# Stacks made by halves, gelus tied to a later split, and two slabs' low parts on VectorE in the differential-attention layer

## The chip, the cores and the metric

The kernel runs on one core of a Trainium2 chip. The metric is the device time of one execution in microseconds (us). PE is TensorE (matrix products), DVE is VectorE, ACT is ScalarE, POOL is GpSimd, and SP is SyncE, which issues the transfers.

## The reference

Two layers over 512 tokens and 256 context tokens, 768 in all, of width 1024. The change lies in the first ("even") layer. After an adaptive norm, `h` is projected into gate streams `u` and `v`, and into queries, keys and values of four heads. The heads are differential: two softmaxes of 64-wide queries and keys are subtracted, and each head's output is normed.

```python
u, v, q, k, vv = jnp.split(h @ w_in, [A_WIDTH, 2 * A_WIDTH, KV_START, KV_START + B_QK_WIDTH], axis=-1)

def diff_attn(q, k, v, lam):
    s = jnp.einsum('bqhd,bkhd->bhqk', q, k).astype(jnp.float32) * ATTN_SCALE
    p = jax.nn.softmax(s, axis=-1).reshape(b, B_HEADS, 2, tq, tk)
    a = p[:, :, 0] - lam * p[:, :, 1]
    return jnp.einsum('bhqk,bkhe->bqhe', a.astype(v.dtype), v)

def diff_out(o, g, lam_init):
    return (rmsnorm(o, g) * (1.0 - lam_init)).reshape(b, t, B_V_WIDTH)
```

The gate branch gives `gelu(u) * mixed(gelu(v))`. Both branches, side by side 1024 wide, go through the output projection `w_out`, and a gated MLP follows. The second ("odd") layer has windowed attention.

## The kernel before

All products are float32 to nearly full precision. Each operand is kept as a high part (a rounded copy, made by ScalarE) and a low part (what is left, a subtraction), and each product is three matmuls: high by high, high by low, low by high (`mm3`, lines 115 to 117). So every operand of PE needs a "split": `split` (L131 the copy on ScalarE, L132 the subtraction on VectorE or GpSimd) for activations, `unit` (L89 the copy, L92 the subtraction) for weights.

`even()` first makes queries, keys and values. Then come the four heads, t = 0 to 3. Each is made by `head(t)` in three passes, qp = 0, 1, 2, over 256 query rows each: `softmax_diff` computes the scores (L546, L547, into the two PSUM buffers of `wide`, called pw), takes the exponential on ScalarE (L550, with row sums) and subtracts the two maps on VectorE; `attend` transposes the map (L567), splits it (tiles ath, atl) and multiplies by the values; ScalarE copies the result into `o` (L579).

Queries and keys of a head are stacked: 64 rows of a high part over 64 of a low part, so that one matmul does the work of two. `stack(t)` made the query stacks (`stack_q`, L272 to L278, tiles qa and qb; the low parts of head 3 on GpSimd) and the key stacks (`stack_k`, L286 to L288, tiles kh and kl) in one go, called in the middle of the previous head, after its pass qp = 1.

While a head's softmax runs on the other engines, PE is filled with projections into a spare PSUM buffer (pf): `block` makes the queries and keys of the heads to come, `gated` the gate streams u, copied to SBUF by L588.

`norm(t, step)` is a head's RMS norm in three steps: squares (L640, tile sq), row sums by PE (L612) and a chain of small VectorE operations on six columns that ends in a diagonal matrix (`head_diag`, L615 to L627, tile q), and a spread of it over all rows (PE, L195) by which `o` is multiplied. For t < 3 the steps lie inside the next head; for head 3 they follow at once.

Behind the heads comes the output projection. `slab(n)` loads 128 rows of its weights (512 KB), in the order of `order = [4, 5, 6, 0, 1, 2, 3, 7]`: heads 0 to 2, the four gate streams, head 3. Slabs 0 and 1 are loaded ahead. The activations `cat[k]` are made by the gelu of a gate stream (k < 4, L671), the multiply by the mixed v, and the split. `project` runs eight slabs over eight 128-column blocks.

A list scheduler with a timeline of its own sets the order of each engine's instructions. `tc.issue_after(x)` makes an instruction stand behind x; `high_priority` puts the heads ahead of the fillers. Before the change `gelu(k)` for k < 4 was tied to the last exponential, `self.last_exp`.

Of the kernel before, what the change touches and what calls it, by code (L numbers as in the profile page):

```python
# [6 lines left out]
F32 = mybir.dt.float32  # L7
F32R = mybir.dt.float32r
# [3 lines left out]
ALU = mybir.AluOpType  # L12
AX = mybir.AxisListType.X

P = 128
# [4 lines left out]
TA = TX + TC  # L20
# [7 lines left out]
class Builder:  # L28
# [99 lines left out]

    def split(self, hi, lo, src, lo_eng=None):
        nc = self.nc  # L130
        nc.scalar.copy(hi, src)  # L131
        return (lo_eng or nc.vector).tensor_tensor(lo, src, hi.bitcast(F32), ALU.subtract)  # L132

    def rstd_small(self, ms, n, inv, tag):
# [133 lines left out]
    def stack_q(self, q, pool, T, tag, bufs, s=1.0, eng=None, out=None):  # L268
# [8 lines left out]
            else:  # L277
                nc.vector.scalar_tensor_tensor(lo[Y], q[X], s, hi[X].bitcast(F32), ALU.mult, ALU.subtract)  # L278
        return qa, qb

    def stack_k(self, k, pool, T, tag, bufs, lows):
        nc = self.nc
        out = []
        for X, Y, kl in zip((slice(0, 64), slice(64, 128)), (slice(64, 128), slice(0, 64)), lows):
            kh = pool.tile([P, T], F32R, name=self.uid("kh"), tag=tag, bufs=bufs)
            nc.scalar.copy(kh[X], k[X])  # L286
            nc.scalar.copy(kh[Y], k[X])
            nc.vector.tensor_tensor(kl[X], k[X], kh[X].bitcast(F32), ALU.subtract)  # L288
            out.append((kh, kl))
        return out  # L290


    def build(self):
# [37 lines left out]
    def even(self):  # L331
        tc, nc, a = self.tc, self.nc, self.a
# [9 lines left out]
        def f3(tag="f3", bufs=4):  # L342
            return R1.tile([P, TA], F32, name=self.uid(tag), tag=tag, bufs=bufs)
# [4 lines left out]
        for k in range(0, KT, 2):  # L348
            t = self.load(Rh, a["xT"][k * P:(k + 2) * P, :].rearrange("(k p) t -> p k t", p=P), [P, 2, TX], f"hx{k}")
# [47 lines left out]
        sq = self.squares(hx, TX)  # L397
# [24 lines left out]
        qk = {}  # L422
# [38 lines left out]
        for k in range(KT):  # L461
            t = self.adap.tile([P, 2, 512], F32R, name=self.uid("wq"), tag="wq", bufs=2) if k in (2, 5) else None
# [8 lines left out]
            t, sh = hx[k], self.modcol(0, 0, k, 0)  # L471
# [31 lines left out]
        for k in range(KT):  # L503
            W = self.unit(a["v0"][k * P:(k + 1) * P, :], 512)
            for tb in range(6):
                c = slice(tb * P, (tb + 1) * P)
# [25 lines left out]
        Ra = tc.alloc_tile_pool(name="att0", bufs=1, side="right", reuse_waits="tile")  # L532
        oraw, raw = [], {}

        def softmax_diff(Q, K, qb, sums):


            koff = 0 if qb < 4 else TX
            qs = slice(qb * P, (qb + 1) * P)
            nm, sums = self.small(2, "sa", 10), sums[:, 2 * qb:2 * qb + 2]  # L540
            es = []
            for c in range(2):
                ps = self.wide()
                for p in range(2):
                    if qb < 4:
                        nc.tensor.matmul(ps[:, :TX], Q[c][:, qs], K[c][p][:, :TX], start=p == 0, stop=p == 1)  # L546
                    nc.tensor.matmul(ps[:, TX:TA], Q[c][:, qs], K[c][p][:, TX:], start=p == 0, stop=p == 1)  # L547
                nc.vector.tensor_reduce(nm[:, c:c + 1], ps[:, koff:TA], axis=AX, op=ALU.max, negate=True)
                e = Ra.tile([P, TA], F32, name=self.uid("e"), tag="e", bufs=6)
                self.last_exp = nc.scalar.activation(e[:, koff:], ps[:, koff:TA], AF.Exp, bias=nm[:, c:c + 1],  # L550
                                                     accum_out=sums[:, c:c + 1])
                es.append(e[:, koff:])
            r = self.small(1, "sa", 10)
            nc.vector.reciprocal(r, sums[:, 1:2])
            nc.vector.scalar_tensor_tensor(r, r, self.nlam, sums[:, 0:1], ALU.mult, ALU.mult)
            nc.vector.scalar_tensor_tensor(es[0], es[1], r, es[0], ALU.mult, ALU.add)
            return es[0]

        def attend(t, Q, K, qp, o, eps):
            es = [softmax_diff(Q, K, 2 * qp + i, eps) for i in range(2)]  # L560
            kbs = list(range(6)) if qp < 2 else [4, 5]
            po = self.bank()[:, :TC]
            for i in range(0, len(kbs), 2):
                pt = self.bank()
                for j in range(2):
                    for b in range(2):
                        nc.tensor.transpose(pt[:, j * TC + b * P:j * TC + (b + 1) * P],  # L567
                                            es[b][:, (i + j) * P:(i + j + 1) * P], self.ident)
                th = Ra.tile([P, 512], F32R, name=self.uid("ath"), tag="at", bufs=6)
                tl = Ra.tile([P, 512], F32R, name=self.uid("atl"), tag="at", bufs=6)  # L570
                self.split(th, tl, pt)
                for j in range(2):
                    kb = kbs[i + j]
                    c = slice(t * P, (t + 1) * P)
                    m = slice(j * TC, (j + 1) * TC)
                    self.mm3(po, (vhi[kb][:, c], vlo[kb][:, c]), (th[:, m], tl[:, m]),
                             i + j == 0, i + j == len(kbs) - 1)
            s = slice(qp * TC, (qp + 1) * TC)
            nc.scalar.copy(o[:, s], po)  # L579

        def gated(i, after=None):

            W = self.blocks(a["uv"][i])
            u = f3() if i < 4 else f3("rv")
            for off, T, A in ((0, TX, axx), (TX, TC, axc)):
                ps = (self.fill if off or i < 4 else self.bank)()[:, :T]
                self.dense(ps, W, A, after, 0 if off else (2, 5)[i == 3])
                nc.scalar.copy(u[:, off:off + T], ps)  # L588
            raw[i] = u

        lows = [[Ra.tile([P, TA], F32R, name=f"kl{i}{c}") for c in range(2)] for i in range(2)]
# [1 line left out]
            nc.gpsimd.memset(lows[i][0][64:128].bitcast(F32), 0.0)  # L593
            nc.gpsimd.memset(lows[i][1][0:64].bitcast(F32), 0.0)

        def stack(t):
            return (self.stack_q(qk[t], Ra, TA, "sq", 3, eng=nc.gpsimd if t == 3 else nc.vector),
                    self.stack_k(qk[4 + t], Ra, TA, "kh", 3, lows[t % 2]))

        norms = {}  # L600

# [31 lines left out]
        def norm(t, step):  # L633

            if t not in norms:
                return
            o, eps = norms[t][:2]
            if step == 0:
                sq = self.sumsq()
                nc.scalar.activation(sq, o, AF.Square)  # L640
                norms[t] = o, eps, sq
            elif step == 1:
                sq = norms[t][2]
                norms[t] = o, eps, head_diag(sq, eps)
            else:
                for off, T, dg in ((0, TX, norms[t][2][0]), (TX, TC, norms[t][2][1])):
                    c = o[:, off:off + T]
                    nc.vector.scalar_tensor_tensor(c, c, self.subg, self.spread(dg), ALU.mult, ALU.mult)

        def head(t):  # L650
            Q, K = QK.pop(t)
            o = f3("o", 4)
            eps = self.small(12, "sx", 2)
            for qp in range(3):
                attend(t, Q, K, qp, o, eps)
                if qp == 0:
                    norm(t - 1, 1)
                elif qp == 1:
                    if t < 3:
                        QK[t + 1] = stack(t + 1)  # L660
                    norm(t - 1, 2)
            norms[t] = o, eps
            norm(t, 0)
            if t == 3:
                norm(t, 1)
                norm(t, 2)
            oraw.append(o)

        def gelu(i, after=None):
            with tc.issue_after(after.ins) if after else ExitStack():  # L670
                return nc.scalar.activation(raw[i], raw[i], AF.Gelu)  # L671
# [34 lines left out]
        def block(n):  # L706
# [7 lines left out]
                evacuate(ps, key, c)  # L714
            self.rope(qk[key][:, :TX], qk[key][:, :TX], tabs)

        QK = {0: stack(0)}
        for g in range(4):
            gated(4 + g)
            last = gelu(4 + g)  # L720
# [11 lines left out]
        for t, jobs in enumerate(((block, 0, 1), (block, 2, 3), (gated, 0, 1), (gated, 2))):  # L732
            for i in jobs[1:]:
                jobs[0](i, *([self.last_exp] if t == 3 else []))
            with tc.high_priority(offset=tc.cur_priority - here), tc.issue_after(last.ins):
                head(t)
        gated(3, self.last_sum)
        Ra.release()
        self.ropep.release()
        self.sh_bufs = 2  # L740
# [9 lines left out]
        def slab(n):  # L750
            k = order[n]
            Ws[k] = self.blocks(a["even_out"][k * P:(k + 1) * P, :], t=slots.pop())

        slab(0)
        slab(1)
        cat = {}
        for k in order:
            if k < 4:
                gelu(k, self.last_exp)
                nc.vector.tensor_tensor(raw[k], raw[k], raw[4 + k], ALU.mult)  # L760
            src = raw[k] if k < 4 else oraw[k - 4]
            cat[k] = self.ax()
            self.split(*cat[k], src, nc.gpsimd if k in (5, 6) else nc.vector)
        Rv.release()
        R1.release()

# [14 lines left out]
        sq, rest = self.sumsq(), []  # L781
# [1088 lines left out]
```

## Time and profile before

| | |
|---|---|
| Three runs | 1573.76, 1575.87 and 1576.09 us; median 1575.87 us |
| Profiled execution | 1582.97 us, of which its span is 1581.2 us |
| PE busy | 1516.2 us, 96% of the span, 9563 matmuls |
| DVE, ACT, POOL busy | 1072.9, 726.4, 828.9 us |
| Stretch of the heads and the first projection weights | about 120 to 360 us of the span |
| Granted clock of PE | 0.99 from 450 us on |

The span is the profiled core's program, and 1.8 us of the profiled time lie around it. A profiled run is one execution; here it lies 7.1 us above the median of the runs. "Granted clock" is the share of full speed that PE's clock had, and "busy" is time in which an instruction was executing.

### The profile page before, as it was taken

The numbers are of one execution on the slowest core, as the hardware profiler recorded it, in microseconds if no ns is written. First come the engines' busy times: TensorE is split into PE (matmuls) and PEld (weight loads), VectorE is DVE, ScalarE is ACT, GpSimd is POOL, SyncE is SP. The second block draws the span as 40 slices with busy tenths as digits, with TensorE's granted clock in tenths as the row PEclk, the third lists the DMA queues.
The fourth block names the chain that finished last, engine by engine and source line by source line (L and its number), as shares of the span: only waits on it lengthen the run. The fifth ranks groups of instructions, "written<-read, shape, count | busy, mean of one in ns | idle before, by whom it ended". The sixth has DMA issues, their size and how long they took to land.

```text
span 1581.2 us, 24961 instructions
## 1 busy us (share of the span) xinstructions
PE 1516.2 (96%) x9563; PEld 1357.0 (86%) x9563; DVE 1072.9 (68%) x1886; ACT 726.4 (46%) x1489; POOL 828.9 (52%) x562
## 2 busy tenths in 40 slices
PE   6999999889999999999999999899999999999998
PEld 4667888779999999999999988777869889999997
DVE  3612778773697787888886487665657976666665
ACT  2415565642562333333333354565655644444444
POOL 0453322051337767767776544531314299898982
PEclk9999999989999999999999999999999999999999
DMA  9762100042123333345442212210224133333301
GB/s 349 293 238 76 44 21 1 1 157 109 68 70 105 108 118 126 128 135 171 163 159 91 81 41 62 69 31 14 68 91 176 53 97 105 99 106 105 99 21 54
DMA packets 53415, 162.26 MB, mean 103 GB/s; under 512 B 6192, under 2 KB 8624, under 8 KB 45616
## 3 DMA queue, kind: packets, MB, share of 16 engines
q1 hardware_dynamic: 46240, 135.37, 25.5%
q10 hardware_dynamic: 7056, 25.30, 4.9%
q8 instruction: 75, 1.23, 0.3%
q14 instruction: 44, 0.36, 0.1%
HBM read 158.55 MB, written 2.10 MB: 102 GB/s over the span
## 4 chain that ended last, share of the span: by engine, by line
PE 84%; DVE 10%; ACT 3%; issue 2%; DMA 0%; POOL 0%; DVEq 0%; SPq 0%; ACTq 0%; POOLq 0%
PE pw L115 11%; PE pw L116 11%; PE pw L117 11%; PE pb L115 9%; PE pb L116 9%; PE pb L117 9%; PE pf L115 4%; PE pf L116 4%; PE pf L117 4%; PE pb L1680 2%; PE pb L1669 2%; PE pf L370 2%; PE pw L1631 1%; PE pw L1639 1%; DVE t L49 1%
## 5 line engine op out<-in xcount | busy, mean ns | idle before, releaser
L92 POOL TENSOR_TENSOR w<-raw,w 128x512 fp32r<-128x512 f32 (+1 forms) x78 | 115.4, 1484 | 239.5 <-ACT w L89 184.2
L116 PE MATMUL pw<-ax,w 128*128 128x384 f32 (+2 forms) x716 | 227.2, 318 | 4.7 <-DVE ax L473 2.5
L828 DVE SCALAR_TENSOR_TENSOR xT<-pb,mod,xT 128x512 f32<-128x512 f32 (+3 forms) x204 | 143.1, 708 | 129.2 <-PE pb L117 128.9
L115 PE MATMUL pw<-ax,w 128*128 128x384 f32 (+2 forms) x716 | 225.9, 318 | 3.6 <-DVE q L49 1.9
L117 PE MATMUL pw<-ax,w 128*128 128x384 f32 (+2 forms) x716 | 227.0, 317 | 0.1
L49 POOL TENSOR_TENSOR w<-raw,w 128x512 fp32r<-128x512 f32 x122 | 186.1, 1541 | 48.5 <-ACT w L49 48.4
L49 POOL TENSOR_TENSOR w<-t,w 128x512 fp32r<-128x512 f32 x99 | 148.1, 1499 | 56.2 <-ACT w L49 56.2
L115 PE MATMUL pb<-hh,w 128*128 128x512 f32 x480 | 171.2, 357 | 2.3 <-DVE xT L828 2.3
L117 PE MATMUL pb<-hh,w 128*128 128x512 f32 x480 | 171.7, 358 | 0.4 <-DVE w L49 0.4
L116 PE MATMUL pb<-hh,w 128*128 128x512 f32 x480 | 171.3, 357 | 0.0
L115 PE MATMUL pw<-T,w 128*128 128x384 f32 (+1 forms) x508 | 157.4, 311 | 2.5 <-DVE hs L1036 1.2
L116 PE MATMUL pw<-T,w 128*128 128x384 f32 (+1 forms) x508 | 157.7, 311 | 1.2 <-DVE T L132 1.2
L117 PE MATMUL pw<-T,w 128*128 128x384 f32 (+1 forms) x508 | 157.6, 311 | 0.0
L115 PE MATMUL pf<-ax,w 128*128 128x256 f32 (+2 forms) x460 | 150.6, 327 | 1.8 <-DVE qf L264 1.1
L116 PE MATMUL pf<-ax,w 128*128 128x256 f32 (+2 forms) x460 | 149.6, 325 | 0.0
L117 PE MATMUL pf<-ax,w 128*128 128x256 f32 (+2 forms) x460 | 149.3, 325 | 0.0
L116 PEld LDWEIGHTS pw<-ax,w 128*128 128x128 f32 x716 | 136.2, 190 | 9.6 <-DVE ax L473 3.4
L115 PEld LDWEIGHTS pw<-ax,w 128*128 128x128 f32 x716 | 135.5, 190 | 8.2 <-DVE q L49 2.6
L117 PEld LDWEIGHTS pw<-ax,w 128*128 128x128 f32 x716 | 136.1, 190 | 2.4 <-DVE w L999 0.4
L49 POOL TENSOR_TENSOR hh<-hs,hh 128x768 fp32r<-128x768 f32 (+1 forms) x42 | 78.1, 1860 | 94.8 <-ACT hh L49 69.1
L49 POOL TENSOR_TENSOR w<-rawo,w 128x512 fp32r<-128x512 f32 x59 | 104.0, 1762 | 29.5 <-ACT w L49 29.5
L240 DVE SCALAR_TENSOR_TENSOR junk<-ar,cb 128x1024 bf16<-128x1024 f32 x64 | 106.7, 1667 | 0.0
(429 smaller groups left out, 3924.9 us busy)
## 6 DMA issues: line engine op xcount, KB each, us to landing
raw<-ffn_in SPq DMA_DIRECT2D x44, 1024.0 KB, 5.1
ar<-ada SPq DMA_DIRECT2D x24, 1024.0 KB, 7.1
ar<-ada ACTq DMA_DIRECT2D x48, 512.0 KB, 3.6
rawo<-ffn_out SPq DMA_DIRECT2D x88, 256.0 KB, 3.0
raw<-odd_out SPq DMA_DIRECT2D x28, 256.0 KB, 2.6
raw<-qk SPq DMA_DIRECT2D x16, 256.0 KB, 4.6
raw<-uv SPq DMA_DIRECT2D x16, 256.0 KB, 3.4
raw<-even_out SPq DMA_DIRECT2D x8, 512.0 KB, 3.6
```

The source lines that it names most:

```text
L49: self.tail[key] = fn(*args, **kw)
L92: eng.tensor_tensor(lo, raw, hi.bitcast(F32), ALU.subtract)
L115: mm(out, s[0], m[0], start=start, stop=False, **kw)
L116: mm(out, s[0], m[1], start=False, stop=False, **kw)
L117: return mm(out, s[1], m[0], start=False, stop=stop, **kw)
L240: return self.nc.vector.scalar_tensor_tensor(junk, t, 1.0, self.cb[who], ALU.mult, ALU.mult, accum_out=self.acc[who][:, col:col + 1])
L370: nc.tensor.matmul(ps[32 * q:32 * q + 32, :w], cst[:, k, :], t[:, w * q:w * q + w], start=k == 0, stop=k == KT - 1, skip_group_check=True)
L828: ins = self.nc.vector.scalar_tensor_tensor(h, ps[:, r], self.modcol(l, j, m, who), h, ALU.mult, ALU.add)
L1631: nc.tensor.matmul(ps[:, st:en], Q, K[g][p][:, b0 * P:b1 * P], start=p == 0, stop=p == 1, skip_group_check=True)
L1639: last = nc.tensor.matmul(ps[:, en:en + TC], Q, K[g][p][:, TX:], start=p == 0 and not edge, stop=p == 1, skip_group_check=True)
L1669: last = nc.tensor.transpose(pt[:, x * P:(x + 1) * P], es[2 * (x % 2) + x // 2][:, kb * P:(kb + 1) * P], self.ident)
L1680: nc.tensor.matmul(po[64 * h:64 * h + 64, :], V[vb][:, 64 * g:64 * g + 64], t[:, h * TC:h * TC + TC], start=kb == 0, stop=kb == nb - 1, sk ...
```

## The change

Three things change in `even()`.

1. `stack_q` and `stack_k` are no longer used there. `stack(t, c)` makes one half, c = 0 or 1, of a head's query and key stacks: three copies on ScalarE (two of keys, one of queries) and two subtractions on VectorE. Half 0 is made in pass qp = 1 of the head before and half 1 in qp = 2, in `attend`, between the softmaxes and the products with the values. All low parts are VectorE's now, head 3's queries too.
2. The gelus for k < 4 are tied to the high part of the split for k = 6 (head 2's output), and the multiplies to the end of `head_diag` of head 3 and to the low part of the split for k = 4.
3. The weights' low parts of slabs 0 and 1 are made by VectorE instead of GpSimd (`self.dve_lo = 1`).

```diff
     def split(self, hi, lo, src, lo_eng=None):
         nc = self.nc
-        nc.scalar.copy(hi, src)
+        self.last_hi = nc.scalar.copy(hi, src)
...
             es = [softmax_diff(Q, K, 2 * qp + i, eps) for i in range(2)]
+            if qp and t < 3:
+                stack(t + 1, qp - 1)
             kbs = list(range(6)) if qp < 2 else [4, 5]
...
-        def stack(t):
-            return (self.stack_q(qk[t], Ra, TA, "sq", 3, eng=nc.gpsimd if t == 3 else nc.vector),
-                    self.stack_k(qk[4 + t], Ra, TA, "kh", 3, lows[t % 2]))
+        def stack(t, c):
+
+            q, k, low = qk[t], qk[4 + t], lows[t % 2][c]
+            X, Y = (slice(0, 64), slice(64, 128))[::1 - 2 * c]
+            qs = Ra.tile([P, TA], F32R, name=self.uid("qs"), tag="sq", bufs=3)
+            kh = Ra.tile([P, TA], F32R, name=self.uid("kh"), tag="kh", bufs=3)
+            nc.scalar.copy(kh[X], k[X])
+            nc.scalar.copy(qs[X], q[X])
+            nc.scalar.copy(kh[Y], k[X])
+            nc.vector.tensor_tensor(qs[Y], q[X], qs[X].bitcast(F32), ALU.subtract)
+            nc.vector.tensor_tensor(low[X], k[X], kh[X].bitcast(F32), ALU.subtract)
+            QK.setdefault(t, []).append((qs, (kh, low)))
...
-                    if t < 3:
-                        QK[t + 1] = stack(t + 1)
                     norm(t - 1, 2)
...
         gated(3, self.last_sum)
+        rooted = self.last_diag
...
+        self.dve_lo = 1
         slab(0)
         slab(1)
+        self.dve_lo = 0
         cat = {}
         for k in order:
             if k < 4:
-                gelu(k, self.last_exp)
-                nc.vector.tensor_tensor(raw[k], raw[k], raw[4 + k], ALU.mult)
+                gelu(k, after)
+                with tc.issue_after(rooted.ins), tc.issue_after(low.ins):
+                    nc.vector.tensor_tensor(raw[k], raw[k], raw[4 + k], ALU.mult)
             src = raw[k] if k < 4 else oraw[k - 4]
             cat[k] = self.ax()
-            self.split(*cat[k], src, nc.gpsimd if k in (5, 6) else nc.vector)
+            ins = self.split(*cat[k], src, nc.gpsimd if k in (5, 6) else nc.vector)
+            if k == 4:
+                low = ins
+            elif k == 6:
+                after = self.last_hi
```

The edit shortens the file ahead of `even()`, so lines behind it carry other numbers in the changed kernel (L550 becomes L539, L579 becomes L570, L671 becomes L669).

ScalarE, at the end of head 3's last pass (qp = 2): e is the exponential, f a gate stream, o the head's output, ath the high part of a transposed map, ax an activation of the projection. Before:

```order
L550 ACTIVATE e_3004,sx_2765<-pw_3000,sa_2993 128x256
L671 ACT_TABLE_LOAD
L671 ACTIVATE f_386_2306<-f_386_2306 128x768
L671 ACTIVATE f_393_2369<-f_393_2369 128x768
L671 ACTIVATE f_476_2711<-f_476_2711 128x768
L579 COPY o_2764<-pb_2808 128x256
L131 CAST ath_2929<-pb_2924 128x512
```

The same place after the change, and behind it the place where the gelus stand now:

```order
L539 ACTIVATE e_3004,sx_2765<-pw_3000,sa_2993 128x256
L570 COPY o_2764<-pb_2808 128x256
L131 CAST ath_2929<-pb_2924 128x512
```

```order
L131 CAST ax_3152<-o_1634 128x768
L131 CAST ax_3156<-o_2017 128x768
L131 CAST ax_3160<-o_2422 128x768
L669 ACT_TABLE_LOAD
L669 ACTIVATE f_386_2306<-f_386_2306 128x768
L669 ACTIVATE f_393_2369<-f_393_2369 128x768
L669 ACTIVATE f_476_2711<-f_476_2711 128x768
L579 COPY f_564_3071<-pf_3098 128x256
L89 CAST w_3138<-raw_3200 128x1024
```

The table load and three gelus have moved from ahead of the copy of `o` to behind the splits of heads 0 to 2, and ahead of the cast of slab 2.

VectorE, in head 3's norm (sm are its small columns, w the weights of a slab). Before:

```order
L615 SCALAR_TENSOR_TENSOR sm_3029<-pb_3033,sm_3031 128x4
L615 SCALAR_TENSOR_TENSOR sm_3029<-pb_3039,sm_3031 128x2
L616 TENSOR_SCALAR sm_3030<-sm_3029 128x6
L617 TENSOR_TENSOR sm_3031<-sm_3030 128x6
L618 SCALAR_TENSOR_TENSOR sm_3031<-sm_3031,sm_3029 128x6
```

After:

```order
L615 SCALAR_TENSOR_TENSOR sm_3029<-pb_3033,sm_3031 128x4
L92 TENSOR_TENSOR w_3143<-raw_3144,w_3143 128x1024
L615 SCALAR_TENSOR_TENSOR sm_3029<-pb_3039,sm_3031 128x2
L616 TENSOR_SCALAR sm_3030<-sm_3029 128x6
L92 TENSOR_TENSOR w_3142<-raw_3148,w_3142 128x1024
L617 TENSOR_TENSOR sm_3031<-sm_3030 128x6
L618 SCALAR_TENSOR_TENSOR sm_3031<-sm_3031,sm_3029 128x6
```

Two low parts of weights stand between the small operations; GpSimd's list no longer has them.

PE, behind the last filler matmuls (pf) that stand between heads 2 and 3; kh, kl, qb and qs are stacks, pb_2588 is head 2's product with the values, pb_2682 head 3's. Before:

```order
L115 MATMUL pf_3072<-ax_321,w_3068 128x512
L116 MATMUL pf_3072<-ax_322,w_3068 128x512
L117 MATMUL pf_3072<-ax_321,w_3068 128x512
L546 MATMUL pw_2890<-kh_2638,qb_2629 128x512
L547 MATMUL pw_2890<-kh_2638,qb_2629 128x256
L546 MATMUL pw_2890<-kl_1044,qb_2629 128x512
L547 MATMUL pw_2890<-kl_1044,qb_2629 128x256
L115 MATMUL pb_2682<-ath_2688,vhi_1022 128x256
```

After:

```order
L115 MATMUL pf_3072<-ax_321,w_3068 128x512
L116 MATMUL pf_3072<-ax_322,w_3068 128x512
L117 MATMUL pf_3072<-ax_321,w_3068 128x512
L116 MATMUL pb_2588<-atl_2610,vhi_1014 128x256
L117 MATMUL pb_2588<-ath_2609,vlo_1015 128x256
L115 MATMUL pb_2588<-ath_2609,vhi_1018 128x256
L116 MATMUL pb_2588<-atl_2610,vhi_1018 128x256
L117 MATMUL pb_2588<-ath_2609,vlo_1019 128x256
L535 MATMUL pw_2882<-kh_2582,qs_2581 128x512
L536 MATMUL pw_2882<-kh_2582,qs_2581 128x256
```

The fifteen filler matmuls stood behind head 3's first scores (pw_2882); they now stand ahead of them and of most of the rest of head 2. The order of `odd()` and of the two MLPs is the same in both kernels.

More of the change, by code (lines that the diff above doesn't have):

```diff
@@ L279, in stack_q @@
         return qa, qb
[L281 to L290, printed above, removed]
     def build(self):
@@ L650, in head @@
         def head(t):
-            Q, K = QK.pop(t)
+            Q, K = zip(*QK[t])
             o = f3("o", 4)
@@ L715, in block @@
             self.rope(qk[key][:, :TX], qk[key][:, :TX], tabs)
-        QK = {0: stack(0)}
+        QK = {}
+        for c in range(2):
+            stack(0, c)
         for g in range(4):
```

## The prediction

> **What bounds the kernel now.** The page comes first: it tells which engine ends last.
>
> ```profile
> span 1581.2 us, 24961 instructions
> PE 1516.2 (96%) x9563; PEld 1357.0 (86%) x9563; DVE 1072.9 (68%) x1886; ACT 726.4 (46%) x1489; POOL 828.9 (52%) x562
> PE 84%; DVE 10%; ACT 3%; issue 2%; DMA 0%; POOL 0%; DVEq 0%; SPq 0%; ACTq 0%; POOLq 0%
> ```
>
> TensorE is busy 96% of the span and makes 84% of the chain that ended last. The change adds and removes no matmul, so it can only act where TensorE waits, or runs at a lowered clock after a wait. The waits of PE in 120 to 450 us, which hold all that the change touches, come next (total, times, longest):
>
> ```profile
> PE pw L546 <- ACT e L550: 5.7, 4, 2.6
> PE pb L115 <- ACT ath L131: 4.7, 3, 3.8
> PE pb L195 <- DVE q L627: 4.2, 1, 4.2
> ```
>
> Then the busy times by stretch (length, then PE, PEld, DVE, ACT, POOL; granted clock; DMA share; GB/s):
>
> ```profile
> 245.00:255.00 10.00, 7.41 (x39) 6.42 (x38) 9.67 (x20) 7.05 (x14) 2.07 (x1) 0.83 0.00 0
> 255.00:300.00 45.00, 44.98 (x291) 40.14 (x290) 33.90 (x68) 26.43 (x57) 5.15 (x3) 1.00 0.00 1
> 300.00:312.00 12.00, 10.91 (x74) 9.06 (x72) 9.37 (x25) 8.07 (x20) 0.00 (x0) 1.00 0.01 1
> 312.00:315.90 3.90, 0.08 (x2) 0.01 (x1) 2.82 (x9) 3.83 (x6) 0.00 (x0) 0.86 0.01 2
> 315.90:323.10 7.20, 7.20 (x31) 6.11 (x32) 4.84 (x11) 1.41 (x3) 0.00 (x0) 0.60 0.00 0
> 334.20:338.45 4.25, 0.02 (x1) 0.00 (x0) 4.15 (x5) 1.80 (x3) 3.26 (x2) 1.00 0.76 271
> 338.45:342.04 3.59, 3.58 (x10) 2.38 (x10) 2.52 (x5) 0.00 (x0) 0.00 (x0) 0.54 0.31 122
> 342.04:360.00 17.96, 17.96 (x105) 17.96 (x105) 11.53 (x6) 10.88 (x13) 15.87 (x6) 1.00 0.66 223
> ```
>
> Two holes stand out, 312.0 to 315.9 and 334.2 to 338.45. Behind each the granted clock is low: 0.60 over 7.20 us and 0.54 over 3.59 us, which is 7.20 × 0.40 = 2.9 and 3.59 × 0.46 = 1.65 us of work lost. From 342.04 on PE is full.
>
> **Part A: the gelus leave the front of ScalarE.** The timeline of the first hole (start, duration):
>
> ```profile
> 311.28 0.19 ACT L550 ACTIVATION_READ_ACCUMULATOR e<-pw,sa 128x1 f32 x1
> 311.47 0.60 PE L567 MATMUL pb<-ident,e 128*128 128x128 f32 x4
> 311.49 1.28 ACT L671 ACT_TABLE_LOAD   x1
> 312.78 2.31 ACT L671 ACTIVATE f<-f 128x768 f32<-128x768 f32 x3
> 315.00 0.35 ACT L579 COPY o<-pb 128x256 f32<-128x256 f32 x1
> 315.25 0.59 ACT L131 CAST ath<-pb 128x512 fp32r<-128x512 f32 x1
> 315.89 0.58 PE L115 MATMUL pb<-ath,vhi 128*128 128x256 f32 x1 [3.82 <-ACT ath L131]
> 316.42 0.68 DVE L132 TENSOR_TENSOR atl<-pb,ath 128x512 fp32r<-128x512 f32 x1
> 323.10 0.60 PE L567 MATMUL pb<-ident,e 128*128 128x128 f32 x4
> ```
>
> The last exponential ends at 311.47; then ScalarE loads the gelu table and runs three gelus, and only afterwards casts the transposed weights for which PE stands. With the gelus tied behind the third split of the output projection, the transposes end at 312.07 and the cast (0.59) releases PE at about 312.75. The wait falls from 3.82 to 0.7 (−3.1). At full clock the 7.20 us shrink by up to 2.9 more, but VectorE is next late: three low parts at 0.68, four small operations and two of L627's before the transposes of 323.10 put these at about 318.0 instead of 317.1, so 0.9 to 1.0 is taken back. A = −3.1 − 2.9 + 0.9 = **−5.1**; bounds −3.1 (no clock comes back) and −6.0.
>
> Shorter waits stand at the starts of two earlier heads:
>
> ```profile
> 212.87 0.79 PE L546 MATMUL pw<-kh,qa 128*128 128x512 f32 x1 [1.94 <-ACT e L550]
> 249.83 0.70 PE L546 MATMUL pw<-kh,qa 128*128 128x512 f32 x1 [2.59 <-ACT e L550]
> ```
>
> The clock was 0.83 in 245 to 255, around the wait of 2.59, so a wait of that length costs clock too; the 0.7 that is left in A is far below it.
>
> [...]
>
> **Part B: VectorE makes the first slabs' low parts.** The second hole, head 3's norm:
>
> ```profile
> 328.49 0.16 DVE L615 SCALAR_TENSOR_TENSOR sm<-pb,sm 128x4 f32<-128x4 f32 x1 [3.44 <-PE pb L612]
> 328.54 4.74 POOL L92 TENSOR_TENSOR w<-raw,w 128x1024 fp32r<-128x1024 f32 x2 [42.92 <-PE pb L612]
> 329.13 1.84 DVE L616 TENSOR_SCALAR sm<-sm 128x6 int32<-128x6 int32 x1
> 331.00 2.29 DVE L617 TENSOR_TENSOR sm<-sm 128x6 f32<-128x6 f32 x1
> 333.33 0.17 DVE L618 SCALAR_TENSOR_TENSOR sm<-sm,sm 128x6 f32<-128x6 f32 x1
> 333.88 3.58 POOL L132 TENSOR_TENSOR ax<-o,ax 128x768 fp32r<-128x768 f32 x2 [0.61 <-ACT ax L131]
> 333.93 1.78 DVE L621 SCALAR_TENSOR_TENSOR sm<-sm,sm 128x6 f32<-128x6 f32 x1
> 335.75 1.73 DVE L622 SCALAR_TENSOR_TENSOR sm<-sm 128x6 f32<-128x6 f32 x1
> 337.71 1.03 DVE L627 SCALAR_TENSOR_TENSOR q<-sm,ident 128x512 f32<-128x512 f32 x2
> 338.45 1.86 PE L195 MATMUL pb<-q,ones 128*128 128x512 f32 x2 [4.23 <-DVE q L627]
> ```
>
> Operations on six columns that take 0.17 elsewhere take 1.84, 2.29, 1.78 and 1.73 while POOL makes a low part: 7.64 − 4 × 0.17 = 7.0 us of blocking on the chain for which PE waits 4.23. With the two slabs' lows on VectorE the first two of these blocks go, and the chain is done before POOL turns to the splits' lows at 333.88. What VectorE pays is bounded by
>
> ```profile
> L288 DVE TENSOR_TENSOR kl<-f,kh 64x768 fp32r<-64x768 f32 x8 | 7.6, 949 | 0.5 <-ACT kh L286 0.3
> L92 POOL TENSOR_TENSOR w<-raw,w 128x1024 fp32r<-128x1024 f32 x8 | 21.5, 2708 | 49.6 <-PE pb L612 42.9 <-ACT w L89 6.6
> ```
>
> VectorE's own subtraction scaled to 1024 columns gives 0.949 × 1024/768 = 1.27 each; POOL's price is 2.71. I take 1.27, the row of the engine that does it. From 328.49: ten small operations (2.0), two lows (2.5) and L627's first (0.7) end at 333.7. PE reaches the spreads at about 334.5, because the order puts them behind the last filler block (334.2) and two projection matmuls (17.96/105 = 0.17 each). So the wait of 4.23 goes, and the 1.65 of clock with it: B = **−5.9**. At POOL's price the chain ends at 333.7 + 2 × 1.44 = 336.6, 2.1 is waited, and B = −(4.23 − 2.1) − 1.65 = −3.8.
>
> [...]
>
> **Part C: the heads' order moves.** The stacks made in halves change PE's order: the last fifteen filler matmuls stand 21 attention matmuls earlier, so the stretch of attention alone is 21 × 44.98/291 = 3.2 us longer. In 300 to 312, with no filler, 12.00 − 10.91 = 1.09 was idle, which scales to 0.3; one whole wait like the 2.59 above is the other end. I take +1.0, between 0 (no gain, since 255 to 300 was full already) and 2.5. Head 3's two query lows go from POOL to VectorE, two at the 0.949 of the row above (the same shape). VectorE is busy 33.9 of 45 there and PE waits for none of it, so 0; if that cover were gone it would cost 1.9.
>
> **Part D: the halves themselves.** ScalarE's copies keep their number and stand at the same place before the first scores of each head, so the two waits above stay: 0.
>
> **Part E: the feed behind the hole.** The gelus must now run after the third split, before the casts of slabs 2 and up.
>
> ```profile
> 332.24 2.30 ACT L131 CAST ax<-o 128x768 fp32r<-128x768 f32 x3 [0.59 <-PE pf L116]
> 342.27 0.37 ACT L588 COPY f<-pf 128x256 f32<-128x256 f32 x1 [6.27 <-PE pf L117]
> 342.55 2.00 ACT L89 CAST w<-raw 128x1024 fp32r<-128x1024 f32 x2
> ```
>
> ScalarE: splits to 334.5, table and gelus 1.28 + 2.31 to 338.1, a copy 0.37, slab 2's cast 1.0 to 339.5, then POOL's 2.71: ready at 342.3. PE starts the projection near 336, behind the two spreads, and two slabs occupy it 2 × 24 × 17.96/105 = 8.2 us, to 344.2. The margin is 1.9 us; afterwards a slab takes PE 4.1 us and POOL 2.71. So 0, as long as that margin holds.
>
> **The sum.** −5.1 − 5.9 + 1.0 + 0 = −10.0. The profiled execution was 1582.97 (1581.2 of span and 1.8 around), so it would be 1573.0 with a span of 1571.2. It lies 7.1 above the median of the runs, 1575.87; the same 10.0 off the median gives **1565.9**. With the bounds of A, B and C together it is 1575.87 − 11.9 = 1564.0 to 1575.87 − 4.4 = 1571.5 (−3.1 − 3.8 + 2.5). A change under 0.2% (3.15 us) can't be told from none.
>
> **The rivals.**
> *Partial* (0.12): the clock doesn't come back, and VectorE's lows cost what POOL's do. A −3.1, B −3.8, C +1.0 = −5.9: 1570.0. For it speaks that VectorE was never seen on a 128x1024 low; against it, that 300 to 312 runs at 1.00 with short waits.
> *Feed* (0.15): VectorE's multiplies and splits and POOL's lows block each other, pair by pair, so a slab costs POOL 2.71 + 0.95 = 3.66 in place of 2.71. Two such before slab 2 use up the margin of 1.9, and B's clock and wait come back as waits in the projection. B is handed back up to −0: −5.1 + 1.0 = −4.1, or 1571.8; half of this case counts as faster, half as within 0.2%. [...]
> *Slower* (0.13): in heads 2 and 3 the longer stretch has only the two buffers of scores, and PE meets the exponentials. A wait costs 2.59 and lowers the clock to 0.83 over 10 us, 1.7 more: 4.3 each. In place of C's 1.0 they eat up A and B (11.0) at 2.6 such waits; from the fourth on it is slower, +17.2 − 11.0 = +6.2, or 1582.1. For it speaks that the 5.7 us on exponentials is the largest wait of the list; against it, that 300 to 312, without filler, lost only 1.09.
>
> **How the numbers follow.** Forecast 0.60, partial 0.12, feed 0.15, slower 0.13. Faster by over 0.2% (under 1572.7): 0.60 + 0.12 + half of 0.15 = 0.80; within: 0.07; slower: 0.13. The range reaches from 1561.5 (the best bound 1564.0 less the 2.3 by which the shown runs differ) to 1573.5 (the feed rival's 1571.8 with 1.7 of its own margin), and leaves out the slower case.
>
> **What would show it.** Right: PE's wait ahead of L115 on the first cast of head 3's last part under 1 us and a clock of 0.9 or more in the 7 us behind it; no wait above 0.5 ahead of the two spreads; L616, L617, L621 and L622 near 0.2; VectorE's lows near 1.27; no wait over 1 us in the first three slabs of the projection. Wrong: waits for exponentials in heads 2 and 3 adding to more than 5.7 + 2.5 us, lows of 2.7 on VectorE, or a projection that stands for slab 2.

## The result and the profile after

The changed kernel takes 1568.30 us, the median of 6 runs (1566.44 to 1569.63), against 1575.98 us for the kernel before (median of 6, 1573.76 to 1578.90): 7.7 us less. The ratio is 0.9950, with a 95% interval of 0.9937 to 0.9963, which is 5.8 to 9.9 us. The forecast was 1565.9 us, 10.0 less, with a range of 1561.5 to 1573.5. The profiled execution took 1569.63 us, 1.3 above the median, where that of before lay 7.1 above its own. The page after:

```profile
span 1567.8 us, 24952 instructions
PE 1513.8 (97%) x9563; PEld 1355.0 (86%) x9563; DVE 1069.2 (68%) x1890; ACT 726.4 (46%) x1489; POOL 820.0 (52%) x558
```

The waits of PE in 120 to 450 us after the change (total, times, longest):

```profile
PE pw L535 <- ACT e L539: 5.0, 3, 2.6
PE pb L116 <- DVE atl L132: 1.9, 4, 0.7
PE pb L699 <- DVE rv L700: 1.7, 1, 1.7
PE pb L115 <- ACT ath L131: 1.4, 2, 0.7
PE pb L612 <- ACT sq L640: 1.3, 1, 1.3
```

The waits of 3.8 for a cast and of 4.2 for the norm's diagonal are gone from the list; what is left stood there before, with one short wait on `atl` more. The timeline of the first hole and of the stretch behind it:

```profile
310.12 0.60 PE L612 MATMUL pb<-ones,sq 128*128 128x128 f32 x4
310.56 0.60 PE L558 MATMUL pb<-ident,e 128*128 128x128 f32 x4
311.20 0.59 ACT L131 CAST ath<-pb 128x512 fp32r<-128x512 f32 x1 [0.51 <-PE pb L558]
311.84 0.39 PE L115 MATMUL pb<-ath,vhi 128*128 128x256 f32 x1 [0.68 <-ACT ath L131]
316.77 0.64 PE L558 MATMUL pb<-ident,e 128*128 128x128 f32 x4
321.00 2.42 PE L612 MATMUL pb<-ones,sq 128*128 128x128 f32 x12 [1.34 <-ACT sq L640]
323.65 0.63 PE L116 MATMUL pf<-ax,w 128*128 128x512 f32 x1
326.96 0.39 PE L115 MATMUL pf<-ax,w 128*128 128x256 f32 x1 [0.67 <-ACT f L579]
```

Three of the same rows in the kernel before:

```profile
311.03 0.61 PE L612 MATMUL pb<-ones,sq 128*128 128x128 f32 x4
327.29 1.60 PE L612 MATMUL pb<-ones,sq 128*128 128x128 f32 x12 [1.34 <-ACT sq L640]
331.70 0.38 PE L115 MATMUL pf<-ax,w 128*128 128x256 f32 x1 [0.73 <-ACT f L588]
```

The cast follows the transposes directly and the wait is 0.68. The last transposes stand at 316.77 in place of 323.10. But the row sums at 321.00 now take 2.42 us where they took 1.60, and filler matmuls 0.63 where they take 0.40: the clock falls here, in a place where it did not fall before. The norm's chain on VectorE:

```profile
322.68 1.23 DVE L92 TENSOR_TENSOR w<-raw,w 128x1024 fp32r<-128x1024 f32 x1
324.01 0.17 DVE L616 TENSOR_SCALAR sm<-sm 128x6 int32<-128x6 int32 x1
325.24 0.16 DVE L617 TENSOR_TENSOR sm<-sm 128x6 f32<-128x6 f32 x1
326.63 1.02 DVE L627 SCALAR_TENSOR_TENSOR q<-sm,ident 128x512 f32<-128x512 f32 x2
330.29 1.46 PE L195 MATMUL pb<-q,ones 128*128 128x512 f32 x4
```

The small operations are at 0.16 to 0.17, a low part costs VectorE 1.23, the diagonals are done by 327.65, and PE comes for them at 330.29 without a wait. The busy times by stretch (length, PE, PEld, DVE, ACT, POOL, granted clock, DMA share, GB/s) show the lowered clock, 0.50 from 321.60 to 325.01, and then a full PE:

```profile
311.00:317.00 6.00, 5.24 (x34) 3.99 (x33) 4.93 (x16) 2.13 (x4) 0.00 (x0) 1.00 0.00 1
318.18:321.60 3.42, 1.74 (x11) 1.34 (x12) 0.57 (x1) 1.87 (x3) 0.00 (x0) 1.00 0.85 335
321.60:325.01 3.41, 3.41 (x15) 3.02 (x14) 2.37 (x5) 1.42 (x2) 0.00 (x0) 0.50 0.40 136
330.30:348.00 17.70, 17.70 (x100) 17.16 (x100) 16.01 (x11) 12.37 (x16) 13.04 (x6) 1.00 0.44 152
```

Two rows that stand in every kernel here, the wait of the mixing matmuls of the v gate streams (called row sums of the gate streams, or of the values, in two expectations below) and the wait for the MLP's first transposed activation, mark the beginning and the end of the stage that the change touches. Before, then after:

```profile
191.55 1.60 PE L701 MATMUL pb<-sq,rv 128*128 128x128 f32 x12 [1.74 <-DVE rv L702]
431.19 0.44 PE L116 MATMUL pw<-T,w 128*128 128x384 f32 x1 [1.16 <-DVE T L132]
```

```profile
190.22 1.60 PE L699 MATMUL pb<-sq,rv 128*128 128x128 f32 x12 [1.74 <-DVE rv L700]
420.34 0.44 PE L116 MATMUL pw<-T,w 128*128 128x384 f32 x1 [1.17 <-DVE T L132]
```

The stage lasts 239.64 us before and 230.12 after: 9.5 less. Within it, by the starts of equal rows: from its beginning to the last row sums of head 2 (L612 x4, 311.03 before, 310.12 after) it is 0.42 longer; from there to head 3's row sums (327.29 and 321.00) 5.38 shorter; from these to the last filler block (331.70 and 326.96) 1.55 longer; and from there to the end 6.1 shorter.

### The profile page after: what moved, and what is told of

Same layout as the page of the kernel before. It is cut to its first block, busy times and chain, and to the rows that moved or that the text cites. A ratio compares the mean times of both kernels' runs of the same rounds, so it can differ in the third digit from the quotient of the medians.

```text
span 1567.8 us, 24952 instructions
## 1 busy us (share of the span) xinstructions
PE 1513.8 (97%) x9563; PEld 1355.0 (86%) x9563; DVE 1069.2 (68%) x1890; ACT 726.4 (46%) x1489; POOL 820.0 (52%) x558
## 3 DMA queue, kind: packets, MB, share of 16 engines
q8 instruction: 75, 1.23, 0.3%
## 4 chain that ended last, share of the span: by engine, by line
PE 85%; DVE 9%; ACT 3%; issue 2%; DMA 1%; POOL 0%; DVEq 0%; SPq 0%; ACTq 0%; POOLq 0%
PE pw L116 11%; PE pw L115 11%; PE pw L117 11%; PE pb L116 9%; PE pb L115 9%; PE pb L117 9%; PE pf L115 4%; PE pf L116 4%; PE pf L117 4%; PE pb L1688 2%; PE pb L1677 2%; PE pf L359 2%; PE pw L1639 1%; PE pw L1647 1%; DVE t L49 1%
## 5 line engine op out<-in xcount | busy, mean ns | idle before, releaser
L92 POOL TENSOR_TENSOR w<-raw,w 128x512 fp32r<-128x512 f32 (+1 forms) x76 | 111.9, 1478 | 202.0 <-ACT w L89 193.1
```

The lines of the kernel that those rows point to most:

```text
L92: eng.tensor_tensor(lo, raw, hi.bitcast(F32), ALU.subtract)
```

## The experiments

The interval of such a difference of medians is 4 to 6 us wide. The traces cut finer, but each is one execution, so the stage is taken in three parts by the starts of equal rows: "heads" up to the last row sums of head 2, "first hole" from there to head 3's row sums, "second hole" from there to the column sums behind the projection (413.08 us in the kernel before, 402.24 after). "Less" is against the kernel before on the same chip, from the ratio and its interval.

| kernel | median, us | less than before, us | heads | first hole | second hole |
|---|---|---|---|---|---|
| before, three profiles | | | 119.48, 119.63, 119.59 | 16.26, 16.27, 16.29 | 85.79, 85.60, 85.60 |
| whole change | 1568.30 | 7.9 (5.8 to 9.9) | 119.90 | 10.88 | 81.24 |
| whole change, again | 1570.83 | 7.4 (4.4 to 10.4) | 119.57 | 10.87 | 81.27 |
| ties alone (A) | 1573.82 | 3.2 (0.9 to 5.5) | 118.22 | 11.02 | 83.14 |
| slab lows on VectorE alone (B) | 1575.72 | 2.8 (0.6 to 5.2) | 119.65 | 16.31 | 79.69 |
| halves alone | 1576.55 | 1.6 (−0.5 to 3.6) | 119.30 | 14.19 | 83.12 |
| A and B, no halves | 1568.76 | 8.5 (5.7 to 11.4) | 119.76 | 11.01 | 81.29 |
| the same, again | 1570.39 | 8.4 (5.4 to 11.4) | 119.64 | 11.03 | 81.29 |
| A and halves, no B | 1574.01 | 4.4 (2.2 to 6.6) | 119.59 | 10.87 | 82.95 |
| filler earlier | 1570.96 | 6.8 (4.7 to 8.8) | 119.51 | 10.87 | 82.37 |
| and two more lows on VectorE | 1569.20 | 8.4 (5.4 to 11.4) | 119.40 | 10.88 | 78.25 |
| and multiplies later | 1576.43 | 0.2 (−2.5 to 3.0) | 118.02 | 10.88 | 86.10 |

The two holes repeat to 0.2 us from profile to profile of one kernel. The heads differ by 1.4 us between kernels that are equal there (119.40 and 118.02 in the last two), so nothing under that is read from them. The profiles with 118.02 and 118.22 hold one stretch of 3.4 us at half the clock in the heads, all the others two or three.

**The ties alone.** On the kernel before, only the gelus and multiplies are tied as in the change.

```diff
-                gelu(k, self.last_exp)
-                nc.vector.tensor_tensor(raw[k], raw[k], raw[4 + k], ALU.mult)
+                gelu(k, after)
+                with tc.issue_after(rooted.ins), tc.issue_after(low.ins):
+                    nc.vector.tensor_tensor(raw[k], raw[k], raw[4 + k], ALU.mult)
```

> Part A alone on the kernel before: the gelus and multiplies tied as in the change, stacks whole, slabs 0 and 1 with GpSimd's low parts. Theory of the sum: the wait of 3.82 us for the cast falls to about 0.7, the clock of 0.60 behind it comes back, together 5.1 to 5.4 us faster, and the wait of about 4.2 for the norm's chain stays. Theory of the partial case: only the wait goes, 3.1 us faster. A third reading, that a hole closed here is given back at the next one: under 1 us faster, with the wait ahead of the spreads grown by as much.

The first hole is 5.24 shorter, as the sum said. But the second, which this edit does not touch by name, is 2.65 shorter too, in spite of the clock, which falls at its beginning as in the whole change (VectorE waits 4.36 us for the row sums, 3.44 in the kernel before). VectorE's and GpSimd's timeline there:

```profile
323.02 0.40 DVE L616 TENSOR_SCALAR sm<-sm 128x6 int32<-128x6 int32 x1
323.45 2.30 DVE L617 TENSOR_TENSOR sm<-sm 128x6 f32<-128x6 f32 x1
326.39 0.17 DVE L621 SCALAR_TENSOR_TENSOR sm<-sm,sm 128x6 f32<-128x6 f32 x1
326.59 0.17 DVE L622 SCALAR_TENSOR_TENSOR sm<-sm 128x6 f32<-128x6 f32 x1
321.02 4.71 POOL L92 TENSOR_TENSOR w<-raw,w 128x1024 fp32r<-128x1024 f32 x2 [37.60 <-ACT w L89]
331.21 3.69 POOL L132 TENSOR_TENSOR ax<-o,ax 128x768 fp32r<-128x768 f32 x2 [5.48 <-ACT ax L131]
```

GpSimd's two low parts still run from 321.02 to 325.73, but the row sums end later (the lowered clock), so part of them passes while the chain has not begun, and only two small operations are longer than 0.17: 0.40 and 2.30. The spreads stand earlier in PE's order and the splits later, so GpSimd's splits come at 331.21, after the chain, and block nothing: L621 and L622 are at 0.17 where they were 1.78 and 1.73. None of the three readings put on record said that closing the first hole would shrink the second; the third said the opposite. This profiled execution took 1567.86 us, the lowest of its twelve and 6.0 below their median, at a mean clock of 0.995 where the others had 0.992 or 0.993. The medians (3.2 us less, 0.9 to 5.5) do not tell the 5.1 to 5.4 of the sum from the 3.1 of the partial case.

**The slab lows alone.**

```diff
+        self.dve_lo = 1
         slab(0)
         slab(1)
+        self.dve_lo = 0
```

> Part B alone on the kernel before: only slabs 0 and 1 have their low parts made by VectorE. Theory of the sum: the four small operations fall from 1.7 to 2.3 us to 0.17 each, the low parts take 1.2 us each, the wait of 4.23 and the clock of 0.54 behind it go, 5.9 to 6.1 us faster. Partial case: 3.8 faster. Feed case: PE waits for slab 2 or 3 and less than 2 us are left.

The first hole is unchanged, the second 5.9 to 6.1 shorter:

```profile
314.44 0.58 PE L115 MATMUL pb<-ath,vhi 128*128 128x256 f32 x1 [3.81 <-ACT ath L131]
325.89 1.60 PE L612 MATMUL pb<-ones,sq 128*128 128x128 f32 x12 [1.34 <-ACT sq L640]
405.58 1.28 PE L170 MATMUL pb<-ones,t 128*128 128x128 f32 x10
```

The forecast's term was 5.9, and it did not come in the medians in full (0.6 to 5.2).

**The halves alone.**

```diff
-        def stack(t):
-            return (self.stack_q(qk[t], Ra, TA, "sq", 3, eng=nc.gpsimd if t == 3 else nc.vector),
-                    self.stack_k(qk[4 + t], Ra, TA, "kh", 3, lows[t % 2]))
+        def stack(t, c):
...
```

> The stacks in halves alone, gelus and slabs as in the kernel before. Theory of the sum: 0 to 2.5 us slower, 1.0 taken. The trace of the changed kernel shows 0.4 us lost between the starts of the two traces' heads and the end of head 3, so 0.4 is expected now. Rival: new waits on exponentials, 4.3 us slower for each.

No wait on an exponential was added (5.4 us in all), so that rival falls. Nor is the part worth nothing by itself: the first hole is 2.1 and the second 2.6 shorter. PE waits 2.46 for the cast instead of 3.82, since more of its work now stands behind the last exponential, the clock behind that wait is halved for 3.4 us in place of 6.8 (matmuls of 0.41 us, and of 0.28 again from 317.82 on), and the norm's chain meets GpSimd's low parts later, as with the ties alone. The medians do not settle whether this reaches the total (−0.5 to 3.6).

**Ties and lows without the halves.** The two edits above together, stacks whole; run on two chips.

> Parts A and B without the halves. If the parts add up: 5.4 + 6.1 = 11.5 less what the trace of the changed kernel lost once behind head 3 (1.55 us of lowered clock), 10 to 11.5 us faster than before, and so 2 to 4 us faster than the whole change (7.7 measured). If the halves pay for themselves by what they let the scheduler do, it is 7.7 or less.

> Parts A and B without the halves, beside the whole change on the same chip. If the halves are worth nothing or cost 0.4 us, the two are equal within 1 us. If they pay, as the 2.1 us of the halves alone could mean, this one is 2 us slower than the whole change; if they cost, as 9.9 against 7.7 could mean, 2 us faster.

On the first chip it is 8.5 us faster than before (5.7 to 11.4), which takes in both readings of the first expectation. Beside the whole change on one chip it takes 1570.39 against 1570.83 us, and the holes are equal within 0.2. With the other two parts in, the halves are worth nothing that these runs can show.

**The low parts on GpSimd again.**

```diff
-        self.dve_lo = 1
+        self.lo_after = rooted
         slab(0)
         slab(1)
-        self.dve_lo = 0
+        self.lo_after = None
```

> The whole change, but the low parts of slabs 0 and 1 stay on GpSimd and are tied behind the end of head 3's norm chain. If GpSimd's subtractions block VectorE's small operations for their whole length, the chain is as fast as in the change (every small operation 0.16 to 0.17 us, no wait of PE for it), and PE waits at the projection's start for the low parts, which end at 2 x 2.7 us behind the chain: up to 1.5 us slower than the change. If the small operations were slow for another reason (the place in the chain, the loads of the weights), they stay at 1.7 to 2.3 us and this one is some 5 us slower.

The tie did not do what it was meant to do: it sets a place in the plan, not a wait between engines, and GpSimd's queue held nothing else. The low parts ran as soon as the casts were there:

```profile
324.87 2.28 DVE L619 TENSOR_TENSOR sm<-sm 128x6 f32<-128x6 f32 x1
322.45 4.68 POOL L94 TENSOR_TENSOR w<-raw,w 128x1024 fp32r<-128x1024 f32 x2 [61.77 <-ACT w L90]
```

So it is the whole change without part B (the file's lines stand two lower), and neither of its two expectations was tested. It says, for these executions, what B is worth when A is in: 1.7 us of the second hole (82.95 against 81.24 and 81.27), and 3.2 of the medians on that chip. Alone, B took 5.9 to 6.1 off that hole and 2.8 off the median.

**The filler ahead of the squares.** Six of the nine filler matmuls held for the norm's chain are released when the last product with the values is issued.

```diff
-        gated(3, self.last_sum)
+        gated(3, self.last_sum, self.last_pv)
...
-            with self.tc.issue_after(after.ins) if after and k >= first else ExitStack():
+            tie = after if k >= first else mid if k >= early else None
+            with self.tc.issue_after(tie.ins) if tie else ExitStack():
```

> The whole change, and six of the filler matmuls that were held back behind head 3's row sums are tied only behind its last product with the values, so that they fill the 1.34 us in which PE waits for the squares. If the wait ends last there and the lowered clock behind it (0.63 instead of 0.40 us for a filler matmul) comes from that pause: 1.3 to 2.9 us faster than the change. If the norm's chain is what ends last, the 1.3 us return as a wait ahead of the spreads and nothing changes.

```profile
320.39 1.60 PE L613 MATMUL pb<-ones,sq 128*128 128x128 f32 x12
330.75 1.13 PE L196 MATMUL pb<-q,ones 128*128 128x512 f32 x2 [1.80 <-DVE q L628]
338.75 0.44 PE L116 MATMUL pb<-ax,w 128*128 128x384 f32 x1 [1.76 <-DVE o L649]
```

```profile
326.38 1.80 DVE L623 SCALAR_TENSOR_TENSOR sm<-sm 128x6 f32<-128x6 f32 x1
328.22 1.75 DVE L624 SCALAR_TENSOR_TENSOR sm<-sm,sm 128x6 f32<-128x6 f32 x1
325.81 4.13 POOL L133 TENSOR_TENSOR ax<-o,ax 128x768 fp32r<-128x768 f32 x2 [66.18 <-ACT ax L132]
```

The pause and the lowered clock are gone together: the row sums take 1.60 again. (Lines such as L613 stand one lower than in the changed kernel, where it is L612.) What was gained came back as two waits, 1.80 and 1.76. The first came because ScalarE reached the splits earlier and GpSimd's two low parts of them fell on the chain: 1.80 and 1.75 for operations of 0.17. The second is for the norm's multiply, which stood behind three multiplies of gate streams; these took 7.10 us beside GpSimd's weights (8.87 for three). The second expectation held in its result (nothing changes); its cause was the block.

**Two more low parts on VectorE.**

```diff
-            ins = self.split(*cat[k], src, nc.gpsimd if k in (5, 6) else nc.vector)
+            ins = self.split(*cat[k], src, nc.vector)
```

> The earlier filler of the run before, and the low parts of the splits of heads 1 and 2 made by VectorE instead of GpSimd. There the 1.3 us of pause and the lowered clock were gone, but two small operations of the norm's chain took 1.80 and 1.75 us while GpSimd made these two low parts, and PE then waited 1.80 and 1.76. If that block ate the gain: the two operations are back at 0.17, VectorE pays 2 x 0.95 for it, the wait ahead of the spreads is under 0.5, and from the first row sums of the values to the end of the projection it takes 1 to 2 us less than the run before and 2 to 3 less than the whole change. If VectorE is the bound there, nothing comes of it: the 1.9 us stand in the chain in their place.

```profile
327.74 0.16 DVE L623 SCALAR_TENSOR_TENSOR sm<-sm 128x6 f32<-128x6 f32 x1
328.69 0.16 DVE L624 SCALAR_TENSOR_TENSOR sm<-sm,sm 128x6 f32<-128x6 f32 x1
330.57 2.69 DVE L765 TENSOR_TENSOR f<-f,rv 128x768 f32<-128x768 f32 x3
332.79 11.98 POOL L92 TENSOR_TENSOR w<-raw,w 128x1024 fp32r<-128x1024 f32 x4 [71.80 <-ACT w L89]
```

Taking GpSimd's work away takes the block away: both operations are back at 0.16, the three multiplies, which now end about when GpSimd begins its weights, take 2.69 in place of 7.10, no wait for the diagonals or for the norm's multiply is left, and the second hole is 78.25, the shortest here, 3.0 below the whole change and 4.1 below the run before, where 1 to 2 were expected. The median (1569.20, 8.4 less than before) can't be told from the whole change's.

**The multiplies later.** The multiplies are tied behind the last multiply of head 3's norm.

```diff
-        rooted = self.last_diag
+        rooted = self.last_norm
```

> As the one above, and the multiplies of the gate streams tied behind the last multiply of head 3's norm rather than behind its diagonal matrix. The wait of 1.76 us for that multiply, which stood behind 7.1 us of multiplies, should go: 1 to 1.8 us less in that stage. Over all some 3 us faster than the whole change, which is 7.5 to 7.7 faster than before; the interval of such a difference is about 2 us, so the trace's stage decides.

```profile
346.63 0.69 PE L117 MATMUL pw<-ax,w 128*128 128x384 f32 x1 [5.60 <-DVE ax L133]
```

```profile
333.14 10.40 DVE L765 TENSOR_TENSOR f<-f,rv 128x768 f32<-128x768 f32 x4
343.47 3.10 DVE L133 TENSOR_TENSOR ax<-f,ax 128x768 fp32r<-128x768 f32 x1
331.13 14.63 POOL L92 TENSOR_TENSOR w<-raw,w 128x1024 fp32r<-128x1024 f32 x5 [71.79 <-ACT w L89]
```

A miss: it was to gain 1 to 1.8 and lost 7.9 in the second hole. Three multiplies that took 2.69 in the kernel above, all but the last 0.5 us of it before GpSimd began its weights at 332.79, now begin at 333.14, after GpSimd, and four take 10.40 beside it; its low parts take 2.93 each (14.63 for five), where two took 4.74 in the kernel before. The first split of a gate stream comes late and PE waits 5.60. This is the mutual block of the prediction's feed rival, made to happen by one line, though what PE waits for is a split on VectorE and not the low part of a slab.

**The kernel before, twice more.**

> The kernel before, unchanged, to see whether its first profiled execution (7.1 us above the median) is typical in the stage that the change touches. If it is, the stretch from the row sums of the gate streams (191.55) to the wait for the MLP's first transposed activation (431.19) lasts 239.6 us again, within 0.5, and the rest of the span differs. If a lowered clock there was chance, it is 3 us shorter, which would explain why the medians moved by 7.6 where this stretch shows 9.5.

> The kernel before a third time. The stretch that the change touches lasted 239.64 and 239.60 us in the first two profiled executions, whose totals lie 4.5 to 7.1 us above the medians. If the norm's chain is sometimes blocked fewer times by GpSimd (as in the kernels with the ties alone and with the halves alone, where it lost one block instead of four), this execution may show a stretch some 3 us shorter; if the stretch is fixed, 239.6 again, and the missing 2 us between the traces and the medians lie elsewhere in the program.

Both holes are as long as the first time, so in the profiled executions the fall of the clock there is no chance; the whole stage lasted 239.60 and 239.58. Their totals were 1581.12 and 1582.92 us, again above the plain runs beside them, whose median was 1576.65 and whose single time was 1578.85. What the stage takes in a plain run is not shown.

## Why the prediction was right

The direction, the two mechanisms and the range held; 7.7 us of the 10.0 came.

**A** was put at −5.1 and measured −5.38 (−5.24 alone). Wait (0.68 for 3.82) and clock (1.00 from 311 to 317, where it was 0.60 behind the wait) did what the rows of before said, with VectorE late next.

**B** was put at −5.9; the stretch from the last filler block on is 6.1 shorter in the whole change and 5.9 to 6.1 with B alone. That the whole change shows the same figure is in part luck: with the other parts in and B left out, the second hole was only 1.7 longer than in the whole change, so the other parts had broken up most of it. Of the two prices for a low part on VectorE the lower end, 1.27, was right (1.23). That GpSimd's block on VectorE is the cause is shown by the runs that only move which engine makes low parts: small operations at 1.80 and 1.75 with two splits on GpSimd, 0.16 with these on VectorE. The run with the low parts on GpSimd again shows it too: 2.28 us for L619 while a low part of GpSimd runs, 0.16 for the same operation, L617, in the changed kernel.

**C and D**, put at +1.0 and 0, measured +0.42 in one profile of the change and within 0.1 of the kernel before in the other, less than the 1.4 by which equal heads differ. No new wait on exponentials came: the slower rival fell, and the list shows 5.0 us for three such waits in place of 5.7 for four.

**E**: the margin held. PE is busy 17.70 of 17.70 behind the spreads, though VectorE's multiplies and GpSimd's weights did meet there. VectorE and GpSimd did lengthen each other as the feed rival has it: with two more low parts on VectorE, three splits of gate streams took 9.32 us beside 11.98 for four low parts of GpSimd, where a split takes 0.95 alone. Its distance was small, as the last edit above shows (10.40 for four multiplies, 5.60 of waiting). No run shows that rival's 3.66, a sum of two rows; in the changed kernel GpSimd's low parts took 3.07 each there (9.20 us for three). The range of the prediction, too, begins at 1561.7 by its own working (1564.0 − 2.3), not at 1561.5.

**What the sum lacked** is the term of +1.55: with the first hole closed, the clock falls at head 3's row sums instead. Part A took 2.9 of lowered clock out of the sum and did not ask where it would fall next. The pauses there (0.68, 0.34 and 1.34 us of PE between 317.4 and 321.0) are the same in the kernel before, where the clock stayed up. The clock of the profiles, cut finely, shows what the fall goes with. In all fourteen of them it is 1.00 or 0.50 and nothing between, and it changes only on a grid of steps of 3.41 us (in the kernel before, its stretches between 212 and 342 us last 3.41, 34.13, 3.41, 61.44, 6.83, 17.07 and 3.41), which does not lie at the same place of the program in every execution (the row sums of the whole change take 2.42 us in one profile and 2.81 in the other). By these numbers a fall costs at least half of 3.41, 1.7 us, where PE has work. The share of a step in which PE was busy goes with what comes next (the first 20 and the last 15 us of each profile are left out). All 61 steps at full clock with a share under 0.46 were followed by half the clock; of 96 between 0.46 and 0.64, 18 were; of some 6000 above, none. The profiles of the kernel before and of the change alone have 8 of 8, 4 of 17 and none of 861. Two steps in the kernel before and one with the earlier filler:

```profile
321.64:325.05 3.41, 2.44 (x14) 1.66 (x13) 1.92 (x3) 0.96 (x2) 0.00 (x0) 1.00 0.10 14
325.05:328.47 3.42, 2.04 (x15) 1.84 (x16) 0.00 (x0) 2.26 (x3) 0.00 (x0) 1.00 0.97 347
```

```profile
317.05:320.47 3.42, 2.66 (x13) 1.91 (x13) 0.69 (x1) 1.67 (x4) 0.00 (x0) 1.00 0.74 252
```

In the changed kernel the pauses of 0.34 and 1.34 fall into one step, which leaves PE 1.74 of 3.42 us (0.51), and the next step runs at 0.50. In the kernel before a new step begins between them (0.72 and 0.60), and with the filler the 1.34 is gone (0.78); no fall follows. So in these profiles the fall goes with what a whole step leaves PE, not with the longest pause, and where the grid lies decides with it; at shares between 0.46 and 0.64 the share alone does not tell.

With it the traces' sum is +0.42 − 5.38 + 1.55 − 6.10 = −9.5. **The step that was wrong by size is the last**: taking a difference of profiled executions off the median of plain runs. The three profiled executions of the kernel before lie 4.1 to 7.1 us above the plain runs beside them, the two of the changed kernel 0.5 and 1.3 above theirs. The mean clock of each run is on record, and the time goes with it: of the 73 plain runs of the kernel before in the experiments, the 10 at 0.990 or less, where its profiles lie, took 1581.5 us on average, and the 6 at 0.994 took 1573.4. So a profiled execution holds its own number of falls of 1.7 us, and not that of the median run: without the first 20 and the last 15 us, eight steps at half the clock in the first profile of the kernel before and six in that of the changed kernel. The interval of 5.8 to 9.9 takes in 9.5; which steps the plain runs lack is not on record, and what separates 9.5 from 7.7 stays open.

**The parts do not add up in the traces**, and the prediction's list of terms hid this. In the two holes A alone takes 7.8 us off, B 5.9 and the halves 4.6; together 9.8. The medians are too wide to show it: 3.2, 2.8 and 1.6 add up to 7.6, against 7.9 for the whole, each within some 2 us. The second hole of the kernel before was a cascade: the first low part delayed the chain (1.84 us for L616), so that the second met it (2.29 for L617), and then both splits did (1.78 and 1.73 for L621 and L622). In the ties alone and in the halves alone the chain's L616 stands 2.0 us behind the start of GpSimd's first low part in place of 0.6, and the blocks cost 2.4 us in place of 7.0. A term is right for the trace that it was read from; the worth of a part depends on what else is in.

## What to carry to other kernels

Look for the same small VectorE operation at 0.17 and at 2 us: here it took 0.15 to 0.17 alone and up to 2.30 beside GpSimd's subtractions. Where it lies on a critical chain, move the large one, or its time, not the chain. When a hole of TensorE is closed, look at the short pauses behind it and add them up: in these profiles the clock fell from 1.00 only behind steps of 3.41 us in which PE was busy for less than 0.64. Such pauses can be filled with matmuls that are held back elsewhere: with six of them in the pause of 1.34, the row sums were back at 1.60 us from 2.42. Look at the mean clock of a profiled execution beside that of the plain runs before its times are taken for theirs. After each such move read who now runs beside whom, since a gain of 3 us and a loss of 8 lay one line apart.

## What was not expected of the hardware

The granted clock halved from 321.60 to 325.01 behind pauses of which none was longer than 1.34 us; two of them fell into one step of the grid and left PE busy for 1.74 of 3.42 us; in the kernel before, with a new step between the same pauses, the clock stayed at 1.00. Operations of VectorE on six columns took between 0.15 and 2.30 us, and multiplies of 768 columns between 0.9 (2.69 for three) and 2.6 (10.40 for four), depending on whether GpSimd was subtracting beside them.
